# Weight differences on GpSimd, Silu at the reload, column-tile loads issued one tile further ahead

## The chip, the cores and the metric

The kernel runs on one core of one Trainium2 chip. The metric is device time in microseconds, the median of several executions. The core has a matrix engine (TensorE, PE in the profile), three elementwise engines (VectorE or DVE, ScalarE or ACT, GpSimd or POOL) and SyncE (SP), whose queue issues nearly all loads and stores between HBM and the on-chip memory SBUF. Each engine takes its own instructions strictly in order; semaphores hold one back until what it needs is there.

## What is computed

The reference is one layer of an encoder on a sequence of 1024 rows of width 1024: a token mixer with four head groups, and then a gated channel mixer (SwiGLU) of hidden width 2816. The change lies in the channel mixer:

```
for l in range(DEPTH):
    ...
    h = rms_norm(x) * (1 + sc1) + sh1
    u = h @ w_in[l]
    ...
    x = x + g1 * y
    h = rms_norm(x) * (1 + sc2) + sh2
    x = x + g2 * ((jax.nn.silu(h @ ffn_w_gate[l]) * (h @ ffn_w_up[l])) @ ffn_w_down[l])
return rms_norm(x, final_norm_g)
```

## The kernel before

The two products of the channel mixer's first half, gate and up, are done together as one two by two block product in the form of Strassen and Winograd: seven products of half-size blocks instead of eight. The hidden width is cut into 22 column tiles of 128 for the gate and 128 for the up weight; the 1024 rows are two blocks of 512 columns in a matmul. Each float32 operand is split into a high and a low part in a TensorE format: the high part is a cast on ACT (L233), the low part a subtraction on VectorE (L239), and one block product is 12 matmuls (hi·hi, hi·lo and lo·hi over four tiles of 128, L1606).

The seven products run in two loops. The **Z loop** (L1653 to L1664) makes the first two, P1 and P1 + P2, for all 22 tiles; ACT copies P1 out (L1661) and applies Silu to P1 + P2 (L1663), and both go to DRAM as psd. The **column loop** (L1716 to L1766) makes the other five for each tile f. It reloads P1 and Silu(P1 + P2) as psr (L1719), makes the weights of tile f + 1 ready, and loads two tiles x and y called sx. For f below 11 these are rows of the down weight wd, whose sums and differences are needed later (L1743, L1751, stored as td); from f = 11 on x holds results stored eleven tiles earlier (s3d, ad), and y is only written.

Making weights ready is `weights(f)`: load wg and wu (two buffers each), form four differences on VectorE (L1673, L1674, L1676, L1678) and split them into T12, T3 and t4s, high and low. The fourth difference is the last to read wg, the split T3l is the last to read wu. The results of PE leave PSUM by VectorE: L1739 and L1741 add P1 to X and Y, L1745 and L1747 add two more products, and after the product with T4 come L1754, the Silu L1755 on ACT and the multiplication L1756. L1749 forms the other half with s1, the Silu read back.

What stands where on each engine is set by a scheduler that knows priorities: `K.first()` puts what is made under it far ahead of the program's order, as far as buffers allow. A tuple of numbers at a tile names the buffers that take turns. So the weights of a tile are split about two tiles before PE uses them. After the column loop follows the down-projection (L1844, products dz, dx, dy).

Lines of the kernel that the text names:

```
def first(self):
    return self.tc.high_priority(offset=2000)
...
def split(self, hi, lo, src, hi_eng="act", lo_eng="dve"):
    ...
        nc.scalar.copy(hi, src)
    ...
    e.tensor_tensor(lo, src, hi.bitcast(F32), op=ALU.subtract)
```

Of the kernel before, what the change touches and what calls it, by code (L numbers as in the profile page):

```python
# [9 lines left out]
F32 = mybir.dt.float32  # L10
F32R = mybir.dt.float32r
AF = mybir.ActivationFunctionType
ALU = mybir.AluOpType
# [4 lines left out]
P = 128  # L18
# [3 lines left out]
NF = 22  # L22
# [263 lines left out]
def build(nc, tc, d, out, dbg=None, dump=None):  # L286
    K = Net(nc, tc, d, out)
    with ExitStack() as es:
# [93 lines left out]
        with ExitStack() as e2:  # L382
            K.pm = psum("pn", e2, m=4)
            lt = pool("lt", e2)

            rpool("edge", e2).tile([P, 120], F32, name="edge")
            rt = rpool("rt", e2)
            sp = Tags(pool("sm", e2))
            S = Slots((lt, 22), (xr, 8), (rt, 20))
            at = attention(K, sp, S)  # L390
            next(at)
            for n, ct in ((2, 6), (0, 0), (1, 4)):
                out_round(K, S, n, ct, n == 2)
            next(at)
            ffn(K, sp, S, at)
# [1186 lines left out]
def ffn(K, sp, S, at):  # L1582
# [4 lines left out]
    nc, d = K.nc, K.d  # L1587
    V = nc.vector
    H, KH = 512, NF // 2
# [11 lines left out]
    def product(ps, w, x, start):  # L1601

        n = 0
        for a, b in ((0, 0), (0, 1), (1, 0)):
            for k in range(4):
                nc.tensor.matmul(ps, lhsT=w[a][:, k], rhs=x[k][b], start=start and n == 0, stop=n == 11, skip_group_check=not start)  # L1606
                n += 1

    def pair(t, slots, name):

        hi, lo = (S.tile([P, NK, P], F32R, s, name + n) for s, n in zip(slots, "hl"))
        K.split(hi, lo, t)
        return [(hi[:, c], lo[:, c]) for c in (slice(0, 4), slice(4, 8))]

    def load(src, f, slot):
        t = S.tile([P, NK, P], F32, slot, src)
        nc.sync.dma_start(t, d[src][f])
        return t
# [36 lines left out]
    for f in range(NF):  # L1655
        with K.first():
            b11, b21 = pair(load("wg", f, W_RAW), (W_HI, W_LO), "wg")
        z = K.pg.tile([P, H], F32, "g", name="Z")
        ps1 = S.tile([P, 2, H], F32, (17, 18, 21), "ps")
        product(z, b11, A["11"], True)  # L1660
        nc.scalar.copy(ps1[:, 0], z)  # L1661
        product(z, b21, A["12"], False)
        nc.scalar.activation(ps1[:, 1], z, AF.Silu)  # L1663
        nc.sync.dma_start(K.psd[f], ps1)  # L1664


    def weights(f):
        wg, wu = load("wg", f, (22, 8)), load("wu", f, (24, 9))
        t12 = S.tile([P, NK, P], F32, (26, 10), "t12")
        t4 = S.tile([P, 4, P], F32, (19, 16), "t4")  # L1670
        B11, B21, B12, B22 = wg[:, 0:4], wg[:, 4:8], wu[:, 0:4], wu[:, 4:8]
        w = {}
        V.tensor_tensor(t12[:, 0:4], B12, B11, op=ALU.subtract)  # L1673
        V.tensor_tensor(t12[:, 4:8], B22, t12[:, 0:4], op=ALU.subtract)  # L1674
        w["T1"], w["T2"] = pair(t12, ((28, 11), (29, 14)), "T12")
        V.tensor_tensor(B12, B22, B12, op=ALU.subtract)  # L1676
        w["T3"], w["22"] = pair(wu, ((20, 12), (23, 15)), "T3")
        V.tensor_tensor(t4, B21, t12[:, 4:8], op=ALU.subtract)  # L1678
        hl = S.tile([P, 2, 4, P], F32R, (25, 13), "t4s")
        K.split(hl[:, 0], hl[:, 1], t4)  # L1680
        w["T4"] = hl[:, 0], hl[:, 1]
        return w


    def wd(k, c):
        return d["wd"][k * P:(k + 1) * P, c * H:(c + 1) * H]

    def operands(n, k):
        a, b = K.ad[k], K.ad[k + KH]
        left, right, less = ((a[:, 0:H], wd(k, 0), None), (K.sd[k][:, 0], K.td[k][:, 1], None),  # L1690
                             (b[:, 0:H], wd(k + KH, 0), None), (K.s3d[k], wd(k + KH, 1), wd(k, 1)),
                             (K.sd[k][:, 1], K.td[k][:, 0], None), (b[:, H:L], wd(k + KH, 0), K.td[k][:, 1]),
                             (K.s4d[k], wd(k + KH, 1), None))[n]
        t = S.tile([P, 2, H], F32, (22, 24, 26, 8, 9), "dr")
        nc.sync.dma_start(t[:, 0], left)
        nc.sync.dma_start(t[:, 1], right)
        if less is not None:
            m = S.tile([P, H], F32, (17, 18, 21), "dm")
            nc.sync.dma_start(m, less)
            V.tensor_tensor(t[:, 1], t[:, 1], m, op=ALU.subtract)  # L1700
        hi = S.tile([P, 2, H], F32R, (28, 20, 25, 11, 12, 13), "dh")
        lo = S.tile([P, 2, H], F32R, (29, 23, 1, 14, 15, 2), "dl")
        K.split(hi, lo, t)
        return hi, lo
# [4 lines left out]
    def more(c=1):  # L1709
        for _ in range(min(c, len(todo))):  # L1710
            with K.first():
                nk = todo.pop(0)
                ops[nk] = operands(*nk)

    with K.first():
        ws = [weights(0)]  # L1716
    for f in range(NF):
        ps1 = S.tile([P, 2, H], F32, (27, 0, 1, 2), "psr")
        nc.sync.dma_start(ps1, K.psd[f])  # L1719
        if f + 1 < NF:  # L1720
            with K.first():
                ws.append(weights(f + 1))
        else:
            more(3)
        x, y = (S.tile([P, 2, H], F32, (17, 18, 21), "sx") for _ in range(2))
        g = f % KH
        if f < KH:
            nc.sync.dma_start(x, d["wd"][f * P:(f + 1) * P].rearrange("p (b e) -> p b e", b=2))
            nc.sync.dma_start(y[:, 0], wd(f + KH, 1))
        else:  # L1730
            nc.sync.dma_start(x[:, 0], K.s3d[g])
            nc.sync.dma_start(x[:, 1], K.ad[g][:, H:L])
        w = ws[f]
        X, Y = (K.pm.tile([P, H], F32, "m", name=n) for n in "XY")
        p1, s1 = ps1[:, 0], ps1[:, 1]
        uv = S.tile([P, 2, H], F32, (3, 4), "uv")
        u, v = uv[:, 0], uv[:, 1]
        product(X, w["T2"], A["S2"], True)
        V.tensor_tensor(u, X, p1, op=ALU.add)  # L1739
        product(Y, w["T1"], A["S1"], True)  # L1740
        V.tensor_tensor(v, Y, p1, op=ALU.add)  # L1741
        if f < KH:
            V.tensor_tensor(x[:, 0], x[:, 1], x[:, 0], op=ALU.subtract)  # L1743
        product(X, w["T3"], A["S3"], False)
        V.tensor_tensor(v, X, v, op=ALU.add)  # L1745
        product(Y, w["22"], A["S4"], False)
        V.tensor_tensor(u, Y, u, op=ALU.add)  # L1747
        a = S.tile([P, L], F32, (5, 6, 7), "a")
        V.tensor_tensor(a[:, 0:H], u, s1, op=ALU.mult)  # L1749
        if f < KH:  # L1750
            V.tensor_tensor(x[:, 1], y[:, 0], x[:, 0], op=ALU.subtract)  # L1751
            nc.sync.dma_start(K.td[f], x)
        product(X, w["T4"], A["22"], False)
        V.tensor_tensor(p1, X, p1, op=ALU.add)  # L1754
        nc.scalar.activation(p1, p1, AF.Silu)  # L1755
        V.tensor_tensor(a[:, H:L], v, p1, op=ALU.mult)  # L1756
        nc.sync.dma_start(K.ad[f], a)
        if f < KH:
            V.tensor_tensor(y[:, 1], a[:, 0:H], a[:, H:L], op=ALU.subtract)
            nc.sync.dma_start(K.s3d[f], y[:, 1])  # L1760
        else:
            V.tensor_tensor(x[:, 0], a[:, H:L], x[:, 0], op=ALU.subtract)
            V.tensor_tensor(x[:, 1], x[:, 1], a[:, H:L], op=ALU.add)
            nc.sync.dma_start(K.sd[g], x)
            V.tensor_tensor(y[:, 0], a[:, 0:H], x[:, 0], op=ALU.subtract)
            nc.sync.dma_start(K.s4d[g], y[:, 0])  # L1766
# [111 lines left out]
```

## Time and profile before

| what | value |
|---|---|
| median of 3 executions | 1514.87 us (1514.78 to 1522.44) |
| profiled execution, its own time | 1520.79 us |
| its span on the core | 1518.9 us |
| mean granted TensorE clock | 0.97 |
| busy: PE, DVE, ACT, POOL | 91%, 74%, 36%, 6% |
| Z loop and column loop, roughly | 820 to 983 us, 983 to 1294 us |
| down-projection to the end | 1294 to 1519 us |

The profiled execution is one of its own, a little slower than the median. Its times place the stages; a difference between two kernels is read from the medians.

### The profile page before, as it was taken

What the parts mean: (1) busy time and instruction counts of PE and PEld (TensorE: products, weight loads), DVE (VectorE), ACT (ScalarE), POOL (GpSimd) and SP (SyncE); (2) the same over time, 40 slices, a digit from 0 to 9 for tenths busy, and PEclk for the clock granted to TensorE, in tenths of its full rate; (3) what the DMA queues carried; (4) which work ended last, traced back from release to release, by engine and by line L of the source; (5) the groups of instructions that cost most, each with busy time, mean ns of one, the idle gap of its engine ahead of it and who ended that gap; (6) DMA issues with size and microseconds to landing.
All of it is one profiled execution on the core that took longest, in us unless ns stands there. A gap on an engine that the chain in (4) does not pass through costs nothing.

```text
span 1518.9 us, 19510 instructions
## 1 busy us (share of the span) xinstructions
PE 1389.5 (91%) x6717; PEld 1115.8 (73%) x6717; DVE 1118.4 (74%) x2123; ACT 542.5 (36%) x973; POOL 90.9 (6%) x143
## 2 busy tenths in 40 slices
PE   2589989998998998999998999999999999999995
PEld 0366768776787767877776777887778878888884
DVE  7999977887756684687865458378777887557588
ACT  2522221232142342333545766322222222434352
POOL 2110000000101231320000000000000000000000
PEclk9789999999998999989999999999999999999998
DMA  6634366577662324476435448677776776977762
GB/s 248 196 101 146 121 198 217 181 240 222 205 195 93 114 84 154 118 250 223 151 102 180 146 164 285 230 258 249 254 246 218 234 266 239 331 236 244 238 221 110
DMA packets 160598, 300.31 MB, mean 198 GB/s; under 512 B 27871, under 2 KB 72831, under 8 KB 160500
## 3 DMA queue, kind: packets, MB, share of 16 engines
q1 hardware_dynamic: 137204, 271.77, 54.6%
q10 hardware_dynamic: 22688, 25.99, 4.8%
q0 software_dynamic: 608, 1.31, 0.3%
q8 instruction: 53, 0.87, 0.2%
q14 instruction: 45, 0.37, 0.1%
HBM read 221.12 MB, written 77.89 MB: 197 GB/s over the span
## 4 chain that ended last, share of the span: by engine, by line
PE 59%; DVE 14%; DMA 9%; issue 3%; ACT 1%; POOL 1%; SPq 0%; POOLq 0%; DVEq 0%; ACTq 0%
PE Z L1606 8%; PE X L1606 6%; PE dx L1844 6%; PE Y L1606 5%; PE gps L495 5%; PE gps L507 4%; PE dz L1844 4%; PE dy L1844 4%; PE gps L1556 3%; DMA mxw<-modw 3%; DMA wu<-wu 2%; PE nS L1429 2%; PE ops L1556 1%; PE nS L1407 1%; DVE wlo L239 1%
## 5 line engine op out<-in xcount | busy, mean ns | idle before, releaser
L495 PE MATMUL gps<-hhi,whi 128*128 128x512 f32 x320 | 130.3, 407 | 3.8 <-ACT nt L531 3.8
L495 PE MATMUL gps<-hlo,whi 128*128 128x512 f32 x320 | 128.9, 403 | 0.0
L495 PE MATMUL gps<-hhi,wlo 128*128 128x512 f32 x320 | 128.4, 401 | 0.0
L239 DVE TENSOR_TENSOR dl<-dr,dh 128x1024 fp32r<-128x1024 f32 x77 | 93.5, 1221 | 37.4 <-ACT dh L233 25.2
L233 ACT CAST dh<-dr 128x1024 fp32r<-128x1024 f32 x77 | 80.4, 1052 | 104.6 <-PE dz L1844 30.0
L1606 PE MATMUL Z<-hp,wgh 128*128 128x512 f32 x352 | 95.8, 402 | 1.0 <-ACT ps L1661 0.9
L507 PE MATMUL gps<-whi,hhi 128*128 128x256 f32 (+1 forms) x256 | 76.8, 300 | 1.5 <-ACT z L531 1.5
L1606 PEld LDWEIGHTS Z<-hp,wgh 128*128 128x128 f32 x352 | 63.6, 188 | 19.2 <-ACT ps L1661 4.7
L507 PE MATMUL gps<-whi,hlo 128*128 128x256 f32 (+1 forms) x256 | 76.8, 300 | 0.0
L507 PE MATMUL gps<-wlo,hhi 128*128 128x256 f32 (+1 forms) x256 | 76.3, 298 | 0.0
L495 PEld LDWEIGHTS gps<-hhi,whi 128*128 128x128 f32 x320 | 60.5, 189 | 19.3 <-ACT nt L531 5.0
L233 ACT CAST T3h<-wu 128x1024 fp32r<-128x1024 f32 x22 | 23.1, 1052 | 132.0 <-PE Y L1606 121.1
L495 PEld LDWEIGHTS gps<-hhi,wlo 128*128 128x128 f32 x320 | 60.2, 188 | 13.7 <-issue 1.6
L495 PEld LDWEIGHTS gps<-hlo,whi 128*128 128x128 f32 x320 | 60.4, 189 | 12.2 <-issue 0.8
L1500 DVE SCALAR_TENSOR_TENSOR mxacc<-mxw,cond,mxacc 128x512 f32<-128x512 f32 x56 | 41.9, 748 | 32.4 <-DMA mxw<-modw 32.2
L1606 PE MATMUL X<-A,t4s 128*128 128x512 f32 x264 | 63.6, 390 | 0.1
L1606 PEld LDWEIGHTS X<-A,t4s 128*128 128x128 f32 x264 | 49.5, 188 | 10.8 <-DVE uv L1745 0.5
L507 PEld LDWEIGHTS gps<-whi,hhi 128*128 128x128 f32 x256 | 49.9, 195 | 3.1 <-ACT z L531 1.9
L1606 PE MATMUL Y<-AS,T3h 128*128 128x512 f32 x176 | 45.5, 400 | 7.3 <-DVE uv L1741 7.3
L1844 PE MATMUL dx<-dh,dl 128*128 128x512 f32 x132 | 51.4, 389 | 0.0
L1844 PE MATMUL dx<-dh 128*128 128x512 f32 x132 | 51.4, 389 | 0.0
L1844 PE MATMUL dx<-dl,dh 128*128 128x512 f32 x132 | 51.4, 389 | 0.0
(521 smaller groups left out, 3511.2 us busy)
## 6 DMA issues: line engine op xcount, KB each, us to landing
wg<-wg SPq DMA_DIRECT2D x44, 512.0 KB
mxw<-modw SPq DMA_DIRECT2D x64, 256.0 KB
raw<-w_in SPq DMA_DIRECT2D x28, 512.0 KB
dr<-wd SPq DMA_DIRECT2D x55, 256.0 KB
psd<-ps SPq DMA_DIRECT2D x22, 512.0 KB
psr<-psd SPq DMA_DIRECT2D x22, 512.0 KB
wu<-wu SPq DMA_DIRECT2D x22, 512.0 KB
ad<-a SPq DMA_DIRECT2D x22, 512.0 KB
```

Of the source, the lines that this page charges most:

```text
L233: nc.scalar.copy(hi, src)
L239: e.tensor_tensor(lo, src, hi.bitcast(F32), op=ALU.subtract)
L495: nc.tensor.matmul(ps, lhsT=w[:, k, c], rhs=x[k][:, t], start=n == 0, stop=n == len(seq) - 1)
L507: nc.tensor.matmul(ps, lhsT=x[k][:, t], rhs=w[:, k, :N], start=n == 0, stop=n == len(seq) - 1)
L1407: nc.tensor.matmul(pb[:, :nk], lhsT=qt[r, i], rhs=ktv[r, r0:r0 + nr, f * 24:f * 24 + 40], start=True, stop=True)
L1429: nc.tensor.matmul(pb[:, 448:512], lhsT=pT[:w * 40, n], rhs=vw[:w * 40, n, c:c + 64], start=n == 0, stop=n == len(chunks) - 1)
L1500: V.scalar_tensor_tensor(acc, in0=mt, scalar=K.cond[:, k:k + 1], in1=acc, op0=ALU.mult, op1=ALU.add)
L1556: K.nc.tensor.matmul(ps, lhsT=l, rhs=r, start=n == 0, stop=n == 5)
L1606: nc.tensor.matmul(ps, lhsT=w[a][:, k], rhs=x[k][b], start=start and n == 0, stop=n == 11, skip_group_check=not start)
L1844: nc.tensor.matmul(acc[i], lhsT=a[:, 0, ts], rhs=b[:, 1], start=first and m == 0, stop=final and m == 2, skip_group_check=n in (2, 3, 5, 6))
```

## The change

Three things. The second half of the Z loop's result is copied and not put through Silu; the column loop applies Silu to it after the reload. The four weight differences are issued on GpSimd in place of VectorE. And the loads are cut out of `weights`: in iteration f the loads of wg and wu of tile f + 2 and of x and y of tile f + 1 are issued, both with priority, where it was those of f + 1 without priority for x and y. The x and y tiles get four buffers of their own in place of three, one of which is taken from psr, which keeps three of four.

```diff
--- before.py
+++ after.py
@@ -1660,22 +1660,25 @@
         product(z, b11, A["11"], True)
         nc.scalar.copy(ps1[:, 0], z)
         product(z, b21, A["12"], False)
-        nc.scalar.activation(ps1[:, 1], z, AF.Silu)
+        nc.scalar.copy(ps1[:, 1], z)
         nc.sync.dma_start(K.psd[f], ps1)


-    def weights(f):
-        wg, wu = load("wg", f, (22, 8)), load("wu", f, (24, 9))
+    def weight_loads(f):
+        return load("wg", f, (22, 8)), load("wu", f, (24, 9))
+
+    def weights(f, wg, wu):
         t12 = S.tile([P, NK, P], F32, (26, 10), "t12")
         t4 = S.tile([P, 4, P], F32, (19, 16), "t4")
         B11, B21, B12, B22 = wg[:, 0:4], wg[:, 4:8], wu[:, 0:4], wu[:, 4:8]
         w = {}
-        V.tensor_tensor(t12[:, 0:4], B12, B11, op=ALU.subtract)
-        V.tensor_tensor(t12[:, 4:8], B22, t12[:, 0:4], op=ALU.subtract)
+        G = nc.gpsimd
+        G.tensor_tensor(t12[:, 0:4], B12, B11, op=ALU.subtract)
+        G.tensor_tensor(t12[:, 4:8], B22, t12[:, 0:4], op=ALU.subtract)
         w["T1"], w["T2"] = pair(t12, ((28, 11), (29, 14)), "T12")
-        V.tensor_tensor(B12, B22, B12, op=ALU.subtract)
+        G.tensor_tensor(B12, B22, B12, op=ALU.subtract)
         w["T3"], w["22"] = pair(wu, ((20, 12), (23, 15)), "T3")
-        V.tensor_tensor(t4, B21, t12[:, 4:8], op=ALU.subtract)
+        G.tensor_tensor(t4, B21, t12[:, 4:8], op=ALU.subtract)
         hl = S.tile([P, 2, 4, P], F32R, (25, 13), "t4s")
         K.split(hl[:, 0], hl[:, 1], t4)
         w["T4"] = hl[:, 0], hl[:, 1]
@@ -1712,17 +1715,9 @@
                 nk = todo.pop(0)
                 ops[nk] = operands(*nk)

-    with K.first():
-        ws = [weights(0)]
-    for f in range(NF):
-        ps1 = S.tile([P, 2, H], F32, (27, 0, 1, 2), "psr")
-        nc.sync.dma_start(ps1, K.psd[f])
-        if f + 1 < NF:
-            with K.first():
-                ws.append(weights(f + 1))
-        else:
-            more(3)
-        x, y = (S.tile([P, 2, H], F32, (17, 18, 21), "sx") for _ in range(2))
+    def sum_loads(f):
+
+        x, y = (S.tile([P, 2, H], F32, (17, 18, 21, 2), "sx") for _ in range(2))
         g = f % KH
         if f < KH:
             nc.sync.dma_start(x, d["wd"][f * P:(f + 1) * P].rearrange("p (b e) -> p b e", b=2))
@@ -1730,9 +1725,31 @@
         else:
             nc.sync.dma_start(x[:, 0], K.s3d[g])
             nc.sync.dma_start(x[:, 1], K.ad[g][:, H:L])
+        return x, y
+
+
+    with K.first():
+        loaded = weight_loads(0)
+        ws = [weights(0, *loaded)]
+        loaded = weight_loads(1)
+        xy = sum_loads(0)
+    for f in range(NF):
+        ps1 = S.tile([P, 2, H], F32, (27, 0, 1), "psr")
+        nc.sync.dma_start(ps1, K.psd[f])
+        x, y = xy
+        g = f % KH
+        if f + 1 < NF:
+            with K.first():
+                ws.append(weights(f + 1, *loaded))
+                if f + 2 < NF:
+                    loaded = weight_loads(f + 2)
+                xy = sum_loads(f + 1)
+        else:
+            more(3)
         w = ws[f]
         X, Y = (K.pm.tile([P, H], F32, "m", name=n) for n in "XY")
         p1, s1 = ps1[:, 0], ps1[:, 1]
+        nc.scalar.activation(s1, s1, AF.Silu)
         uv = S.tile([P, 2, H], F32, (3, 4), "uv")
         u, v = uv[:, 0], uv[:, 1]
         product(X, w["T2"], A["S2"], True)
```

The rows that follow stand in the order of one engine's queue, each with its line, its tiles (numbered when they are made) and, in brackets, for whose semaphores it waits. Line numbers of after differ: psr load L1738 (was L1719), x L1723 and y L1724 (L1728, L1729), differences L1676, L1677, L1679, L1681, L1756 (L1739), L1758 (L1741), L1760 (L1743), L1762 (L1745), L1764 (L1747), L1766 (L1749), L1768 (L1751), L1771 (L1754), L1772 (L1755), L1773 (L1756), stores L1769, L1774, L1777, L1781, L1783 (L1752, L1757, L1760, L1764, L1766); L1752 is the new Silu.

SP's queue in the first half of the column loop, before:

```order
L1719 DMA psr_9460<-psd6_162 128x1024 [waits DMAHW7_49,Activation_49]
L1728 DMA sx_9273<-wd 128x1024 [waits DMAHW6_49,DMAHW0_49]
L1617 DMA wg_9567<-wg 128x1024 [waits DMAHW1_49,DVE_49]
L1752 DMA td3_181<-sx_9168 128x1024 [waits DMAHW3_49,DVE_49]
L1617 DMA wu_9464<-wu 128x1024 [waits DVE_49]
L1729 DMA sx_9274<-wd 128x512 [waits DMAHW4_49,DMAHW2_49]
L1757 DMA ad3_133<-a_9228 128x1024 [waits DMAHW5_49,DVE_49]
L1760 DMA s3d3_203<-sx_9169 128x512 [waits DVE_49]
```

and of the change:

```order
L1617 DMA wu_9283<-wu 128x1024 [waits DVE_49]
L1723 DMA sx_9285<-wd 128x1024 [waits DMAHW6_49,DMAHW4_49]
L1774 DMA ad2_132<-a_9134 128x1024 [waits DVE_49]
L1777 DMA s3d2_202<-sx_8968 128x512 [waits DMAHW0_49,DVE_49]
L1617 DMA wg_9493<-wg 128x1024 [waits DMAHW1_49,Pool_49]
L1738 DMA psr_9368<-psd5_161 128x1024 [waits DMAHW2_49,Activation_49]
L1724 DMA sx_9180<-wd 128x512 [waits DMAHW3_49,DMAHW0_49]
L1769 DMA td4_182<-sx_9179 128x1024 [waits DVE_49]
L1617 DMA wu_9389<-wu 128x1024 [waits DMAHW5_49,DVE_49]
```

The wg load waited for VectorE and now waits for POOL; the psr load and the load of y (L1724) have moved behind it.

VectorE's queue over one tile in the first half, before:

```order
L1739 TENSOR_TENSOR uv_9384<-X_9382,psr_9355 128x512 [waits PE_49]
L1673 TENSOR_TENSOR t12_9571<-wu_9569,wg_9567 128x512 [waits DMAHW3_49,DMAHW1_49]
L1759 TENSOR_TENSOR sx_9274<-a_9333 128x512 [waits DMAHW2_49,DVE_49]
L1674 TENSOR_TENSOR t12_9571<-wu_9569,t12_9571 128x512 [waits DVE_49]
L239 TENSOR_TENSOR T12l_9471<-t12_9466,T12h_9470 128x1024 [waits PE_49,Activation_49]
L1676 TENSOR_TENSOR wu_9569<-wu_9569 128x512
L1678 TENSOR_TENSOR t4_9572<-wg_9567,t12_9571 128x512 [waits DVE_49]
L1741 TENSOR_TENSOR uv_9384<-Y_9383,psr_9355 128x512
L1751 TENSOR_TENSOR sx_9378<-sx_9379,sx_9378 128x512 [waits DMAHW4_49]
L1745 TENSOR_TENSOR uv_9384<-X_9382,uv_9384 128x512 [waits DVE_49,PE_49]
L1747 TENSOR_TENSOR uv_9384<-Y_9383,uv_9384 128x512 [waits PE_49]
L239 TENSOR_TENSOR T3l_9476<-wu_9464,T3h_9475 128x1024 [waits Activation_49]
```

and of the change:

```order
L1756 TENSOR_TENSOR uv_9186<-X_9183,psr_9156 128x512 [waits PE_49]
L1760 TENSOR_TENSOR sx_9285<-sx_9285 128x512 [waits DMAHW6_49,DMAHW4_49]
L1758 TENSOR_TENSOR uv_9186<-Y_9184,psr_9156 128x512 [waits PE_49]
L239 TENSOR_TENSOR T12l_9269<-t12_9264,T12h_9268 128x1024 [waits Activation_49]
L1762 TENSOR_TENSOR uv_9186<-X_9183,uv_9186 128x512 [waits DVE_49,PE_49]
L1768 TENSOR_TENSOR sx_9179<-sx_9180,sx_9179 128x512 [waits DMAHW3_49]
L1764 TENSOR_TENSOR uv_9186<-Y_9184,uv_9186 128x512 [waits PE_49]
L239 TENSOR_TENSOR T3l_9274<-wu_9177,T3h_9273 128x1024 [waits Activation_49]
L1766 TENSOR_TENSOR a_9240<-uv_9186,psr_9156 128x512 [waits DMAHW7_49,DVE_49]
L1771 TENSOR_TENSOR psr_9156<-X_9183,psr_9156 128x512 [waits PE_49]
L239 TENSOR_TENSOR t4s_9278<-t4_9265,t4s_9278 128x512 [waits Activation_49]
```

The four differences and the wait of the first for wu and wg are gone; L1768, which waits for the load of y of the next tile, stands ahead of L1764 and T3l, as L1751 stood ahead of L1747. That is so in tiles 2 to 4 and 6 to 8; in the other tiles of the first half but the first L1768 stands behind T3l.

ACT's queue over one tile in the second half, before:

```order
L233 CAST T3h_10315<-wu_10304 128x1024 [waits DMAHW3_49,PE_49,Activation_49]
L233 CAST t4s_10320<-t4_10307 128x512 [waits PE_49,Activation_49]
L1755 ACTIVATE psr_10195<-psr_10195 128x512 [waits DMAHW6_49,DVE_49]
L233 CAST T12h_10415<-t12_10411 128x1024 [waits PE_49,Activation_49]
L233 CAST T3h_10420<-wu_10409 128x1024 [waits DMAHW3_49,PE_49,Activation_49]
```

and of the change:

```order
L233 CAST T12h_10328<-t12_10324 128x1024 [waits PE_49,Pool_49]
L233 CAST T3h_10333<-wu_10237 128x1024 [waits DMAHW2_49,PE_49,Pool_49]
L1752 ACTIVATE psr_10428<-psr_10428 128x512 [waits DMAHW1_49,DVE_49]
L233 CAST t4s_10338<-t4_10325 128x512 [waits PE_49,Pool_49]
L1772 ACTIVATE psr_10216<-psr_10216 128x512 [waits DVE_49]
```

The new Silu, of psr two tiles ahead, stands ahead of the cast t4s and of the Silu of P1 (L1772, before L1755) and waits for a load. SP's queue there, of the change:

```order
L1617 DMA wg_10447<-wg 128x1024 [waits DMAHW5_49,Pool_49]
L1783 DMA s4d0_211<-sx_9922 128x512 [waits DMAHW6_49,DVE_49]
L1726 DMA sx_10133<-s3d2_202 128x512 [waits DMAHW7_49,DMAHW4_49]
L1727 DMA sx_10133<-ad2_132 128x512 [waits DMAHW0_49]
L1738 DMA psr_10322<-psd14_170 128x1024 [waits DMAHW1_49,Activation_49]
L1617 DMA wu_10343<-wu 128x1024 [waits DMAHW2_49,DVE_49]
```

psr stands behind wg, which waits for POOL, a store and the two loads of x.

## Rows read from the trace of the kernel before

**Rows 1.** Busy time, share and instructions by engine; POOL's busy tenths in 40 slices.

```profile
PE 1389.5 (91%) x6717; PEld 1115.8 (73%) x6717; DVE 1118.4 (74%) x2123; ACT 542.5 (36%) x973; POOL 90.9 (6%) x143
...
POOL 2110000000101231320000000000000000000000
```

**Rows 2.** Chain that ended last: start, us, engine or transfer.

```profile
1082.83 4.15 DMA wu<-wu
...
1096.98 4.93 DMA wu<-wu
...
1111.93 4.62 DMA wu<-wu
...
1294.23 29.92 PE dz L1844 x132
```

**Rows 3.** PE's timeline at the fourth product of tiles 0, 11 and 21.

```profile
990.55 2.00 PE L1606 MATMUL Y<-AS,T3h 128*128 128x512 f32 x8
...
1150.43 2.11 PE L1606 MATMUL Y<-AS,T3h 128*128 128x512 f32 x8 [0.35 <-DVE uv L1741]
...
1288.63 1.98 PE L1606 MATMUL Y<-AS,T3h 128*128 128x512 f32 x8
```

**Rows 4.** Waits from 979 to 1300: us in total, times, longest.

```profile
PE Y L1606 <- DVE uv L1741: 7.3, 9, 1.2
DVE t L1673 <- DMA wu<-wu: 7.0, 9, 1.2
```

**Rows 5.** VectorE's timeline in a tile of the first half.

```profile
1095.63 1.22 DVE L239 TENSOR_TENSOR T3l<-wu,T3h 128x1024 fp32r<-128x1024 f32 x1
...
1102.00 0.69 DVE L1673 TENSOR_TENSOR t<-wu,wg 128x512 f32<-128x512 f32 x1 [1.06 <-DMA wu<-wu]
...
1106.15 0.68 DVE L1741 TENSOR_TENSOR uv<-Y,psr 128x512 f32<-128x512 f32 x1
```

**Rows 6.** SP's timeline, three loads in a row, and VectorE at their last reader.

```profile
1001.96 0.33 SPq L1617 DMA_DIRECT2D wg<-wg  x1
...
1002.83 0.42 SPq L1728 DMA_DIRECT2D sx<-wd  x1
...
1008.32 0.69 DVE L1743 TENSOR_TENSOR sx<-sx 128x512 f32<-128x512 f32 x1 [0.76 <-DMA sx<-wd]
```

**Rows 7.** POOL's groups by line: count, busy us, mean ns, idle before.

```profile
L239 POOL TENSOR_TENSOR hlo<-tm,hhi 128x512 fp32r<-128x512 f32 x8 | 11.9, 1492 | 47.3 <-DVE hhi L235 47.3
...
L429 POOL TENSOR_TENSOR acc<-acc,pr 128x512 f32<-128x512 f32 x7 | 10.1, 1449 | 13.6 <-ACT pr L427 13.3
L1349 POOL TENSOR_TENSOR mhh<-mtt,mnd 128x512 f32<-128x512 f32 x8 | 9.2, 1152 | 44.8 <-DVE mnd L1347 44.8
```

**Rows 8.** Timelines of POOL and VectorE where two subtractions overlap.

```profile
74.16 1.64 POOL L239 TENSOR_TENSOR hlo<-tm,hhi 128x512 fp32r<-128x512 f32 x1 [0.70 <-DVE hhi L235]
...
74.60 2.28 DVE L239 TENSOR_TENSOR wlo<-raw,whi 128x1024 fp32r<-128x1024 f32 x1
```

**Rows 9.** ACT's groups by line: count, busy us, mean ns, idle before.

```profile
L1755 ACT ACTIVATE psr<-psr 128x512 f32<-128x512 f32 x22 | 13.9, 633 | 3.3 <-DVE psr L1754 2.4
L233 ACT CAST t4s<-t 128x512 fp32r<-128x512 f32 x22 | 13.7, 621 | 55.0 <-PE X L1606 54.9
L1663 ACT ACTIVATE ps<-Z 128x512 f32<-128x512 f32 x22 | 13.1, 593 | 3.2 <-PE Z L1606 3.1
L1661 ACT COPY ps<-Z 128x512 f32<-128x512 f32 x22 | 12.9, 585 | 9.0 <-issue 6.1 <-PE Z L1606 1.3 <-ACT ps L1663 1.0
...
L1663 ACT ACT_TABLE_LOAD x6 | 7.7, 1283 | 0.1
```

**Rows 10.** Windows: length, busy us (instructions) by engine, granted clock, DMA share, GB/s.

```profile
806.00:808.00 2.00, 2.00 (x12) 2.00 (x12) 1.89 (x5) 0.28 (x2) 0.00 (x0) 0.50 0.71 291
...
860.00:880.00 20.00, 20.00 (x109) 15.63 (x107) 8.50 (x30) 11.26 (x28) 0.00 (x0) 1.00 0.26 93
1060.00:1080.00 20.00, 17.86 (x78) 14.14 (x77) 15.45 (x23) 3.46 (x5) 0.00 (x0) 1.00 0.75 246
```

**Rows 11.** PE's timeline ahead of the windows at half clock.

```profile
802.38 0.65 PE L1421 MATMUL nT<-ident,nsb 128*120 128x128 f32 x4 [3.15 <-ACT nsb L1417]
```

## The prediction

> **What bounds the kernel now.** First the busy shares [rows 1]: TensorE (PE) is busy 91% of the span, VectorE (DVE) 74%, GpSimd (POOL) 6%, and POOL's line of slices is empty from the middle on, so where the change puts work on POOL nothing else runs there. Then the chain that ended last [rows 2]: the down-projection runs 132 matmuls in 29.92 us, 0.2267 us each, which is what PE needs when nothing holds it up. A column tile has five products of 12 matmuls, so at that rate it takes 60 × 0.2267 = 13.6 us. The timeline of PE at the fourth product of a tile [rows 3] shows what a tile takes: from tile 0 to tile 11 1150.43 − 990.55 = 159.9 us, where 11 × 13.6 = 149.6 would do, and from tile 11 to tile 21 138.2 where 136.0 would do. So the column loop, the only place that the change reaches with any weight, loses about 10.3 us in its first half and 2.2 in its second. That is the whole prize: 12.5 us, 0.8% of the time.
>
> The waits [rows 4] and VectorE's timeline [rows 5] say what loses it. PE waits nine times for the copy-out L1741, 7.3 us in all; VectorE waits nine times for wu at L1673, 7.0 us. VectorE runs its instructions in order: T3l (to 1096.85) frees the wu buffer, wu is loaded in 4.93 us [rows 2], L1673 starts at 1102.00, and only behind it and the rest of the differences stands L1741 (1106.15), for which PE waits. That is a loop one tile long, 14.5 to 15 us, a little over PE's 13.6.
>
> **The change part by part.** *Silu.* At L1663 a Silu of 593 ns becomes a copy like that of L1661, 585 ns [rows 9], and six table loads of 1.28 us go. They buy nothing: in that stage PE is busy 20.00 of 20 us [rows 10], so ACT's time lies beside full products. In the column loop ACT gets a Silu per tile, priced by L1755 at 633 ns; ACT is busy 3.46 of 20 us there [rows 10], so its length is hidden. Its place is not: it waits for a load, and t4s and the Silu of L1772 are queued behind it.
>
> *Differences.* Four instructions of 0.68 us per tile leave VectorE (2.7 of about 11.6 us), and the wait for wu leaves with them. So the old loop is gone. On POOL the same form (128x512 float32, two full operands) shows 1.449 us in the mean at L429; the least of the bounds is 1.152, the mean of L1349, and at the other end L239 with 1.492 [rows 7], stretched where it meets VectorE to 1.64 [rows 8]. I take 1.45, the nearest row: 5.8 us per tile, bounds 4.6 to 6.6. POOL has 13.6 us for it, so its throughput does not bind. What counts is who is queued behind the last of them.
>
> *Loads one tile ahead.* The buffers are still two for wg and two for wu, so a load issued earlier in the program does not start earlier: it waits in SP's queue for its buffer, and everything after it on SP waits too. The rows of the order, in the section on the change, show what: wg of tile f+3 now waits for POOL, because the fourth difference is the last to read the old wg; behind it stand psr and the second wd load, y; and VectorE meets y at L1768 before it gets to L1764 and to T3l, which frees the next wu. So a new loop closes in the first half, one tile long:
>
> T3l ends; 0.1 us to the issue; wu 4.6 us [rows 2]; four differences 5.8; wg, psr and y land. Of three loads issued together, 1.25 MB, the last reader started 6.4 us after the first issue [rows 6], one load alone takes 4.6 to 4.9; I take 5.7 between them, 4.9 where y stands directly behind wg. Then L1768, L1764 and T3l, 0.68 + 0.68 + 1.22 = 2.6. Sum 0.1 + 4.6 + 5.8 + 5.7 + 2.6 = 18.8 us, against 13.6 for PE (18.0 in the short form).
>
> The loop acts only where L1768 of the next tile stands before T3l, which by the order is in two runs of three tiles, 2 to 4 and 6 to 8. A run has some slack before PE feels it: T3l ends nominally 24 matmuls, a copy-out and itself after the third product began (5.4 + 0.7 + 1.2 = 7.3 us), and from there to the next tile's third product six VectorE instructions (4.0 us) are needed, 11.3 of 13.6, so 2.3 us once per run. A run costs (18.0 − 13.6) + 2 × (18.8 − 13.6) − 2.3 = 12.5 us. Two runs: 25.0. At the start of the column loop x of tile 0 is queued on SP behind a wg that waits for POOL, which I estimate at 2.5 us from the same terms. First half: 27.5 lost instead of 10.3, **+17.2**.
>
> In the second half no y is loaded, but psr is, and it stands behind wg, the s4d store and two x loads. ACT's new Silu waits for psr, and t4s and L1772 wait behind it. That closes a loop two tiles long: 0.1 + wu 4.6 + POOL 5.8 + wg to psr landed (1.75 MB; the slope between one load and three gives 6.9 to 7.4, taken 6.9) + Silu 0.63 + t4s 0.62 + L1772 0.63 + five VectorE instructions 3.4 + 7.3 to the next T3l = 30.0 us, 15.0 per tile. Against 13.6 that is 1.4 × 9 tiles = 12.6, less the 2.3 of slack, instead of 2.2: **+8.1**.
>
> The down-projection and everything before the column loop keep their order; nothing is added for them. Sum +25.3: from the median of 1514.87 to **1540**. The profiled execution took 1520.79 (span 1518.9) and was the slow side of the three runs, so a profile of the change as slow as that one would show 1546.
>
> *A page against the rows.* A VectorE subtraction of 1.22 us elsewhere took 2.28 where it overlapped a subtraction on POOL that itself took 1.64 [rows 8]: the two hold each other up. The Trainium skill, page SBUF — State Buffer, section Who interferes with whom, says that a VectorE instruction with two SBUF inputs and a GpSimd instruction that reads SBUF share one port as an exclusive lock, the later one blocking fully; the row agrees in sign, and by that rule rival 3 follows.
>
> **Rivals.** 1. *The other side: the new loop closes inside PE's time.* Only 4.2 us per load (the shortest in [rows 2] is 4.15), 4.6 for the differences and 4.2 for y give 0.1 + 4.2 + 4.6 + 4.2 + 2.6 = 15.7, and the slack of 2.3 then covers a run almost wholly; the second loop gives 26.5, below 27.2. Then the 12.5 us of stalls go but for some 2.5 at the start: 1505. The mechanism is that VectorE no longer stands in front of L1741 waiting for wu; for it speaks that VectorE then needs about 9 of 13.6 us. It decides below about 14.5 us of the one-tile loop. Against it: 5.7 is nearer to the measured three loads than 4.2. Chance 0.22.
>
> 2. *Stalls exchanged.* A loop of 16.5 to 17 us costs 4 to 6 per run, 10 to 12 in the first half, and the second half is where it was: 1510 to 1520, 1515 in the middle. Chance 0.18.
>
> 3. *The lock.* POOL's differences are stretched by VectorE's subtractions to 1.64 and more, and T3l and T12l by POOL's as in [rows 8]. With 7.0 instead of 5.8, and 0.8 more in T3l, the loop is 20.8, a run costs 18.5, the second loop 31.8: about 37 + 2.5 − 10.3 + 18.4 − 2.2 − 2.3 = +43, 1558. For it: VectorE remains busy with two-input subtractions two thirds of the time. Against it: copy-outs read PSUM and one SBUF operand, and the 1.449 is a mean with VectorE at work. Chance 0.12.
>
> 4. *The clock.* After PE had stood for 3.15 us [rows 11] the granted clock was 0.50, 1.2 GHz, in the following windows [rows 10]. The stalls I expect are 4 to 5 us long where the loop acts; each could cost some 3.5 us more over 7 us at half rate. Before, stalls of 1.2 us left the clock at 1.00 [rows 10]. This comes on top of the forecast: with 6 such stalls 1561. Chance 0.08.
>
> **How the numbers follow.** Forecast (1523 to 1550) 0.4; rival 1 0.22; rival 2 0.18; rivals 3 and 4 together 0.2. A measurement of this kernel can tell about 0.5%, 7.6 us, from no change: 1507.3 to 1522.4 is the same. Faster 0.22 (rival 1), same 0.18 (rival 2), slower 0.6 (the rest). The range for 8 in 10 leaves out the lower half of rival 1 and the upper half of rivals 3 and 4: 1505 to 1558. The likeliest case, slower, has its own range of 1523 to 1558.
>
> **What would show it.** Right: four POOL instructions per tile at 1.3 to 1.6 us; SP waiting at L1617 for POOL; VectorE waiting at L1768 for the wd load, several us, in two runs of three tiles with tiles of 17 to 19 us between them; ACT waiting at L1752 for psr in the second half, tiles near 15; PE waiting for L1756, L1762 or L1764; the 29.92 us of the down-projection unchanged. L1673's wait must be gone from VectorE. Wrong: if y lands before VectorE comes to L1768 (then rival 1), if PE's tiles are 13.6 in both halves, if the POOL instructions are over 2 us, or if time is lost in the stage before the column loop, where copies replace Silu.

## The result and the profile after

The changed kernel takes 1585.01 us in the median of six executions, the kernel before, measured beside it, 1517.15. One of the six was disturbed (3483.98); the other five lie between 1581.75 and 1585.93, their median is 1584.22, and the ratio leaves the sixth out: 1.0434, 95% interval 1.0411 to 1.0458. Slower was forecast, but 1540, and at most 1558. The profiled execution took 1585.79, its span is 1584.0, 65.1 longer than before.

The busy times of the page, and POOL's slices [rows 1]:

```profile
PE 1412.1 (89%) x6717; PEld 1130.7 (71%) x6717; DVE 1106.6 (70%) x2035; ACT 543.5 (34%) x988; POOL 228.8 (14%) x231
...
POOL 2110000000103213300000032333334330000000
```

Two numbers stand out. PE is busy 22.6 us longer for the same 6717 matmuls: it ran slower. And VectorE lost 88 instructions of 0.68 us, 60 us, but is busy only 11.8 us less: the rest got 48 us longer.

PE's timeline at the fourth product of tiles 0, 11 and 21, as in [rows 3], and at the third and fourth of tile 12:

```profile
990.96 1.98 PE L1606 MATMUL Y<-AS,T3h 128*128 128x512 f32 x8
...
1177.36 1.98 PE L1606 MATMUL Y<-AS,T3h 128*128 128x512 f32 x8
...
1192.17 3.75 PE L1606 MATMUL X<-AS,T3h 128*128 128x512 f32 x8 [3.77 <-DVE uv L1756]
...
1197.42 2.11 PE L1606 MATMUL Y<-AS,T3h 128*128 128x512 f32 x8
...
1349.58 1.98 PE L1606 MATMUL Y<-AS,T3h 128*128 128x512 f32 x8
```

The first half of the column loop takes 186.4 us where it took 159.9 [rows 3]; the second 172.2 where it took 138.2. With 4.1 more from there to the second product of the down-projection that is nearly the whole difference. The windows of the two halves (columns as in [rows 10]), before and then after, show how much of it is slower work:

```profile
990.55:1150.43 159.88, 152.68 (x662) 123.13 (x661) 127.10 (x185) 36.98 (x44) 0.00 (x0) 1.00 0.73 250
1150.43:1288.63 138.20, 137.43 (x599) 112.02 (x600) 110.81 (x158) 33.73 (x40) 0.00 (x0) 1.00 0.70 239
...
990.96:1177.36 186.40, 160.79 (x662) 129.14 (x660) 118.69 (x143) 41.67 (x55) 69.01 (x45) 0.95 0.61 217
1177.36:1349.58 172.22, 148.60 (x605) 119.44 (x604) 115.87 (x130) 38.31 (x49) 45.87 (x29) 0.92 0.55 196
```

Of the 26.5 us lost in the first half 8.1 are PE's longer busy time, of the 34.0 in the second 11.2; the rest is waiting. After the stall of 3.77 us at 1192.17 a product of 12 matmuls takes 5.25 us (to 1197.42), where 2.72 is PE's own rate. The windows around it, and one further on, show the clock that goes with it:

```profile
1180.00:1200.00 20.00, 16.23 (x61) 12.90 (x60) 11.50 (x13) 4.04 (x6) 6.85 (x4) 0.83 0.46 167
...
1194.00:1196.00 2.00, 2.00 (x6) 1.60 (x5) 0.86 (x1) 0.00 (x0) 1.99 (x1) 0.50 0.00 0
...
1280.00:1300.00 20.00, 15.93 (x58) 12.94 (x59) 13.47 (x15) 3.00 (x5) 5.04 (x4) 0.75 0.50 179
```

0.50 is the lower of the clock's two levels, 1.2 GHz in place of 2.4; the windows of 20 us mix the two.

Three waits that were forecast are there (from 979 to 1365, columns as in [rows 4]): ACT's for psr (28.7 of its 98.5 us between 1175 and 1330, in the second half), PE's for L1756 and VectorE's for y.

```profile
ACT psr L1752 <- DMA psr<-psd: 98.5, 18, 12.8
...
PE X L1606 <- DVE uv L1756: 47.8, 16, 6.8
DVE sx L1768 <- DMA sx<-wd: 35.1, 9, 7.0
```

So is the loop forecast for the first half. Rows of SP, POOL and VectorE from one T3l to the next:

```profile
1054.07 0.33 SPq L1617 DMA_DIRECT2D wu<-wu  x1
...
1057.61 1.27 POOL L1676 TENSOR_TENSOR t<-wu,wg 128x512 f32<-128x512 f32 x1 [11.96 <-DMA wu<-wu]
...
1061.95 2.28 POOL L1681 TENSOR_TENSOR t<-wg,t 128x512 f32<-128x512 f32 x1
...
1064.26 0.33 SPq L1617 DMA_DIRECT2D wg<-wg  x1
...
1069.66 0.69 DVE L1768 TENSOR_TENSOR sx<-sx 128x512 f32<-128x512 f32 x1 [5.99 <-DMA sx<-wd]
1070.27 0.68 DVE L1764 TENSOR_TENSOR uv<-Y,uv 128x512 f32<-128x512 f32 x1
1070.87 1.21 DVE L239 TENSOR_TENSOR T3l<-wu,T3h 128x1024 fp32r<-128x1024 f32 x1
...
1072.12 0.33 SPq L1617 DMA_DIRECT2D wu<-wu  x1
```

wu lands 3.5 us after its issue, the four differences take 6.6, wg to y 5.4, the rest 2.5: 18.05 us from wu to wu, where 18.8 was forecast. In the second half psr stands on the chain that ended last every second tile, as the forecast loop of two tiles has it:

```profile
1197.94 5.11 DMA psr<-psd
...
1209.05 1.74 DVE sx L1782
...
1211.54 4.47 PE X L1606 x12
...
1232.36 5.58 DMA psr<-psd
...
1269.22 5.46 DMA psr<-psd
```

But two tiles take 34.4 and then 36.9 us, where 30.0 was forecast. Rows of VectorE and then of POOL from there show what was not forecast:

```profile
1205.64 1.79 DVE L1779 TENSOR_TENSOR sx<-a,sx 128x512 f32<-128x512 f32 x1
1207.35 1.78 DVE L1780 TENSOR_TENSOR sx<-sx,a 128x512 f32<-128x512 f32 x1
1209.05 1.74 DVE L1782 TENSOR_TENSOR sx<-a,sx 128x512 f32<-128x512 f32 x1
1210.71 0.68 DVE L1756 TENSOR_TENSOR uv<-X,psr 128x512 f32<-128x512 f32 x1
...
1205.59 1.28 POOL L1676 TENSOR_TENSOR t<-wu,wg 128x512 f32<-128x512 f32 x1 [9.60 <-DMA wu<-wu]
1206.95 1.62 POOL L1677 TENSOR_TENSOR t<-wu,t 128x512 f32<-128x512 f32 x1
```

wu lands when VectorE is between L1773 and L1756, and the three subtractions there take 1.74 to 1.79 us each in place of 0.68. L1756, for which PE waits, is 3.3 us later for that alone. L1756 itself keeps its 0.68, though POOL's four differences go on beside it to 1211.92: it reads one operand from PSUM and only one from SBUF.

### The profile page after: what moved, and what is told of

Same layout as the page of the kernel before. It is cut to its first block, busy times and chain, and to the rows that moved or that the text cites. A ratio compares the mean times of both kernels' runs of the same rounds, so it can differ in the third digit from the quotient of the medians.

```text
span 1584.0 us, 19585 instructions
## 1 busy us (share of the span) xinstructions
PE 1412.1 (89%) x6717; PEld 1130.7 (71%) x6717; DVE 1106.6 (70%) x2035; ACT 543.5 (34%) x988; POOL 228.8 (14%) x231
## 5 line engine op out<-in xcount | busy, mean ns | idle before, releaser
L1606 PE MATMUL Z<-hp,wgh 128*128 128x512 f32 x352 | 98.5, 411 | 4.5 <-ACT ps L1661 4.3
L1606 PE MATMUL X<-AS,T3h 128*128 128x512 f32 x176 | 58.8, 489 | 47.8 <-DVE uv L1756 47.8
L1676 POOL TENSOR_TENSOR t<-wu,wg 128x512 f32<-128x512 f32 x22 | 31.9, 1452 | 477.5 <-DMA wu<-wu 318.9
L1606 PEld LDWEIGHTS X<-AS,T3h 128*128 128x128 f32 x176 | 40.6, 240 | 63.2 <-issue 48.9
L239 DVE TENSOR_TENSOR wgl<-wg,wgh 128x1024 fp32r<-128x1024 f32 x22 | 28.1, 1280 | 38.2 <-ACT wgh L233 36.1
```

The source lines that it names most:

```text
L1676: G.tensor_tensor(t12[:, 0:4], B12, B11, op=ALU.subtract)
```

## The experiments

Theory A: SP's queue stands still at the wg load until GpSimd has done its fourth difference, and psr and y stand behind it. Theory B: GpSimd's reads hold up VectorE's subtractions. Rival C: the earlier loads and the third psr buffer do the harm. Rival D: ACT's new wait for psr does. Each time below is a median in us, with its ratio to the kernel before, measured beside it (1516 to 1520), and the 95% interval of the ratio.

**One part at a time.** Loads alone, that is the change with Silu back in the Z loop and the differences back on VectorE:

```diff
-        nc.scalar.copy(ps1[:, 1], z)
+        nc.scalar.activation(ps1[:, 1], z, AF.Silu)
...
-        G = nc.gpsimd
+        G = nc.vector
...
-        nc.scalar.activation(s1, s1, AF.Silu)
```

> Only the loads are issued one tile earlier (with the buffers that this takes); differences stay on VectorE, Silu stays at the Z loop. Theory A (the time is lost because wg waits for GpSimd and psr and y stand behind it): no GpSimd, so no such wait: 1510 to 1525 us. Theory B (GpSimd's reads hold up VectorE's subtractions): the same, 1510 to 1525. Rival C (the earlier loads and the third psr buffer alone do the harm): 1550 or more.

Measured: 1517.80, 0.9985 (0.9965 to 1.0005). The loads by themselves cost nothing. Next the differences alone, the kernel before with `nc.gpsimd.tensor_tensor` in the four lines:

> Only the four differences go to GpSimd; loads and Silu as before. The order still has wg waiting for GpSimd and psr and the second wd load behind it. Theory A: most of the loss is here, 1550 to 1580 us. Theory B: VectorE's stretched instructions come too, 1550 to 1580. Rival C: 1510 to 1525, since the loads are not moved.

Measured: 1574.92, 1.0373 (1.0348 to 1.0398), as both theories have it. Silu alone, at the reload:

> Only the Silu moves from the Z loop to the reload. Theories A and B: 1512 to 1520 us, no difference; TensorE is busy all the time in the Z loop, and with four psr buffers the reload is early. Rival D (ACT waiting for psr in front of t4s is a loss by itself): 1525 or more.

Measured: 1518.94, 1.0018 (0.9991 to 1.0044). The change with `G = nc.vector`:

> The whole change, but the four differences on VectorE. Theories A and B: nearly all of the 68 us come back, 1510 to 1530 us. Rival C: 1550 or more.

Measured: 1520.11, 1.0026 (1.0007 to 1.0045). C and D fall: all but 2 or 3 us of the loss go with the differences' engine. Alone in the kernel before that engine costs 57 us, in the change 65: the moved loads, which cost nothing by themselves, seem to add some 8 to it.

**The reads by themselves.** The base is the kernel before with `(27, 0, 1), "psr"`:

> The kernel before with three psr buffers in place of four, and nothing else: the base for the next two. Both theories: 1513 to 1523 us.

Measured: 1518.77, 0.9988 (0.9958 to 1.0018). On this base, work on GpSimd that no instruction of the column loop waits for:

```diff
         nc.sync.dma_start(K.ad[f], a)
+        idle = S.tile([P, H], F32, 2, "idle")
+        for _ in range(4):
+            nc.gpsimd.tensor_tensor(idle, a[:, 0:H], a[:, H:L], op=ALU.subtract)
```

> The base, and in each column tile GpSimd subtracts the two halves of a four times into a buffer that nobody reads, once a is done. No load waits for these. Theory A (the queue behind the wg load): 1513 to 1525 us. Theory B (GpSimd's reads hold up VectorE's two-input subtractions, some 3 us per tile): 1555 to 1590, with VectorE's 128x512 subtractions at 1.7 us in place of 0.68 where they overlap.

Measured: 1633.64, 1.0761 (1.0717 to 1.0804), 44 us above theory B's range. And the same with fills in place of the four subtractions:

```diff
+        nc.gpsimd.tensor_tensor(idle[:, 0:8], a[:, 0:8], a[:, H:H + 8], op=ALU.subtract)
+        for _ in range(11):
+            nc.gpsimd.memset(idle, 0.0)
```

> As the one before, but GpSimd only fills the buffer, eleven times per tile, about as long, after one subtraction of 8 columns that sets the moment. It writes and hardly reads. Theories A and B: 1513 to 1525 us, VectorE's subtractions at 0.68 us. If VectorE is stretched here too, it is not the reading.

Measured: 1516.80, 0.9986 (0.9960 to 1.0012). VectorE's order in the column loop is the same in both. Timeline of POOL and VectorE in the run with reads:

```profile
1114.85 6.36 POOL L1760 TENSOR_TENSOR idle<-a 128x512 f32<-128x512 f32 x4 [12.52 <-DVE a L1756]
...
1116.61 1.78 DVE L1762 TENSOR_TENSOR sx<-a 128x512 f32<-128x512 f32 x1
1118.31 1.77 DVE L1674 TENSOR_TENSOR t<-wu,t 128x512 f32<-128x512 f32 x1
1120.01 1.75 DVE L1676 TENSOR_TENSOR wu<-wu 128x512 f32<-128x512 f32 x1
```

and in the run with fills:

```profile
1110.38 6.37 POOL L1761 MEMSET idle<- 128x512 f32 x11
...
1112.82 0.68 DVE L1763 TENSOR_TENSOR sx<-a 128x512 f32<-128x512 f32 x1
1113.42 0.68 DVE L1674 TENSOR_TENSOR t<-wu,t 128x512 f32<-128x512 f32 x1
```

POOL is about as long at work in both, 6.7 us per tile with reads and 6.4 with fills in the mean. Only the reads lengthen VectorE, by 1.1 us per subtraction, and four reads per tile cost 115 us, more than the change. Most of the held-up subtractions stand between the copy-outs L1739 and L1741, and PE waits for L1741, with reads and then with fills:

```profile
PE Y L1606 <- DVE uv L1741: 60.4, 15, 4.2
...
PE Y L1606 <- DVE uv L1741: 8.2, 8, 1.6
```

PE's busy time with reads is 1434.3 us, 45.5 more than in the base, for the same matmuls.

**The queue by itself.** psr, x and y of the change by `nc.scalar.dma_start`:

> The whole change, with psr, x and y loaded by ACT's queue, so that they no longer stand behind the wg load; the differences stay on GpSimd. Theory A: the loop through the queue is open, 1520 to 1540 us, and VectorE's wait at L1768 is gone. Theory B: VectorE stays stretched, 1550 to 1575.

Measured: 1554.45, 1.0223 (1.0187 to 1.0259). VectorE's wait at L1768 is gone (0.4 us in all), as theory A has it, but the time lies in theory B's range. The same with `G = nc.vector`:

> As the run with ACT's queue, but the differences on VectorE: neither the reads of GpSimd nor the queue. Against that run (1554 us) this is the price of GpSimd's work without the queue: theory B says 30 to 45 us, so 1510 to 1524. If the rest of the loss were ACT's loads and the Silu: 1540 or more.

Measured: 1535.21, 1.0114 (1.0076 to 1.0152), outside both ranges: ACT's queue costs about 15 us of its own (1520.11 with the same loads on SP's), so this pair shows only that GpSimd costs 19 there, where it costs 65 on SP's queue. Next, psr with priority and `xy = sum_loads(f + 1)` ahead of the weight loads:

> The whole change, with psr loaded with priority and x and y issued in the program before wg and wu: in the order psr now stands ahead of the wg load everywhere, while y still stands behind it, but VectorE comes to y (L1768) mostly after T3l. Theory A for the queue's part: most of the 30 us that ACT's queue gave back come back here too, 1550 to 1565 us; the rest, from GpSimd's reads, stays. If the queue's part is all at y: 1575 or more.

Measured: 1596.01, 1.0517 (1.0474 to 1.0560), more than the change itself. The order was not the expected one: psr was ahead of wg, but in the first half wu now stood behind y, y behind an s3d store and that behind wg; SP waited 131 us for GpSimd. So this run does not say where the queue's part lies. Only the fourth difference on GpSimd (`nc.gpsimd` in that line, `G = nc.vector` for the others):

> The whole change, but only the fourth difference on GpSimd, three on VectorE. Theory B: one read per tile instead of four, about a quarter of the held-up time, 1523 to 1540 us. Theory A alone (wg waits for GpSimd in any case, only the sum of the loop is shorter): 1520 to 1530.

Measured: 1540.52, 1.0133 (1.0093 to 1.0174), just above theory B's range and clear of theory A's. A quarter of the reads costs 20 us of the 65. Three wg buffers, `load("wg", f, (22, 8, 2))`, on the change, for which x and y go back to three:

> The whole change with three wg buffers (x and y go back to three). The wg load then waits for the fourth difference of the tile before, long done, so nothing on SP stands still for GpSimd, while GpSimd reads as much as before. If the loss is mostly the queue: 1525 to 1545 us. If it is mostly the held-up subtractions: 1560 or more. The wait of SP's L1617 for GpSimd should fall from 85 us to under 20 either way.

Measured: 1581.14, 1.0392 (1.0355 to 1.0430). And on the differences alone, with three psr buffers:

> Only the differences on GpSimd, with three wg buffers (and three of psr): loads and Silu as before. Against the run with the differences alone (1575 us): if the queue is most of it 1520 to 1545, if the held-up subtractions are 1555 or more.

Measured: 1575.07, 1.0356 (1.0327 to 1.0385). Both times lie in the range that was to speak for the subtractions, but neither tells the theories apart: the loads were only issued one tile earlier, and SP waited as before. Its wait (us, times, longest) in the run on the change:

```profile
SPq L1617 <- POOL t L1681: 93.5, 18, 7.7
```

In the change it is

```profile
SPq L1617 <- POOL t L1681: 84.9, 18, 8.7
```

The wait without the reads, eleven `nc.gpsimd.memset(B21, 0.0)` behind the fourth difference on VectorE:

> The change with its differences on VectorE, and GpSimd then fills the half of wg that the fourth difference has read, eleven times, before the next wg load may start: the wait of SP for GpSimd without the reads. (The filled data are used by nothing.) In the order psr and y stand ahead of the wg load here, stores behind it. If any wait of SP for GpSimd is dear: 1545 or more. If it is dear only with psr or y behind it: 1520 to 1535.

Measured: 1521.32, 1.0032 (1.0002 to 1.0063). SP waits for GpSimd 27.5 us, and nothing is lost against the change with its differences on VectorE (1520.11). But this wait is a third of the change's, and psr and y stand ahead of the wg load here. No run has them behind it, as in the change, without GpSimd's reads. Last, the wait taken off SP while the reads stay:

```diff
-        return load("wg", f, (22, 8)), load("wu", f, (24, 9))
+        wg = S.tile([P, NK, P], F32, (22, 8), "wg")
+        nc.gpsimd.dma_start(wg, d["wg"][f])
+        return wg, load("wu", f, (24, 9))
```

> The whole change, with the wg loads of the column loop issued by GpSimd itself, right behind its fourth difference. SP's order is that of the change without the wg loads, so nothing on SP waits for GpSimd, while GpSimd reads as in the change. If the loss is mostly SP's queue standing still: 1525 to 1545 us, no wait of SP for GpSimd and none of several us at L1768. If it is mostly the held-up subtractions: 1555 or more, with VectorE's subtractions as long as in the change. The time between them is the share of each.

Measured: 1547.35, 1.0189 (1.0121 to 1.0257). VectorE's busy time, 1102.8 us, is nearly that of the change, so the reads still hold it up. SP's longest waits are now

```profile
SPq L1617 <- DVE T3l L239: 67.2, 19, 8.1
SPq L1700 <- DVE dl L239: 46.3, 27, 4.6
```

and for GpSimd it waits only 5.8 us, at loads of the down-projection. The time lies between the two stated cases, so both causes have a share: 1585 − 1547 = 38 us for the queue; 1547 − 1520 (all on VectorE) = 27 us for the reads. The interval of this run makes each uncertain by some 10 us.

**A third wu buffer.** The kernel before, with `load("wu", f, (24, 9, 2))` and three psr buffers:

> The kernel before with three wu buffers in place of two and three psr buffers in place of four; differences on VectorE. If the wait for wu at L1673 is what holds L1741 up, it goes, and the column loop loses 7 to 10 us: 1507 to 1511 us against 1518. If something else is late by as much: 1515 to 1520.

Measured: 1511.17, 0.9959 (0.9933 to 0.9984), less than either kernel. PE's timeline:

```profile
1099.44 1.98 PE L1606 MATMUL X<-AS,T3h 128*128 128x512 f32 x8
1113.04 1.98 PE L1606 MATMUL X<-AS,T3h 128*128 128x512 f32 x8
1126.64 1.98 PE L1606 MATMUL X<-AS,T3h 128*128 128x512 f32 x8
```

A tile of the first half is 13.60 us, PE's own rate, and of the 7.3 us for which PE waited at L1741 [rows 4] 0.2 are left; a tile of the second half is 13.9, as before. By the medians 8.5 us are won, by the interval 2 to 10, of the 12.5 that the column loop had to give.

## Why the prediction was right and wrong

*What bounds the kernel* was right: a third wu buffer removes the loop through L1673, and the first half of the column loop, where that loop cost most, then runs at 13.6 us. *Silu and its table loads* were worth nothing, as said. *The first-half loop* was right in its links and nearly in its length, 18.05 us for 18.8: shorter loads made up for longer differences. Its price was forecast at 17.2 us over before and is 26.5. From tile 0 to tile 2 the kernel lost 10.0 us, at 17.9 and 19.3 a tile, where 2.5 was allowed for the start; the rest of the half lost 26.8, where the two runs of the forecast lose 25.0.

*The step that failed* is the sum for the second half: forecast +8.1, measured +34.0. A loop two tiles long with psr in it was there, but the sum has "five VectorE instructions 3.4", at 0.68 each. Three of them, L1779, L1780 and L1782, stand where wu lands and POOL starts to read. In seven tiles they took 30.4 us (rows below) where 21 × 0.68 = 14.3 would do: 16 us more. Another 11.2 are PE's slower products. 8.1 + 16 + 11.2 = 35 comes near the 34.0; that these terms simply add is an estimate.

The lock had been put into a rival with a chance of 0.12, on a row that showed it (2.28 for 1.22, [rows 8]). There it stretched only T3l and the differences in the sum, and T12l without a price. T3l was hardly touched, T12l took 1.80 us in place of 1.22, and the subtractions ahead of L1756 were left out. By line, VectorE's mean in the change from 990 to 1310 (columns as in [rows 7]):

```profile
L239 DVE TENSOR_TENSOR T12l<-t,T12h 128x1024 fp32r<-128x1024 f32 x19 | 34.3, 1803 | 0.0
L239 DVE TENSOR_TENSOR T3l<-wu,T3h 128x1024 fp32r<-128x1024 f32 x19 | 23.1, 1217 | 4.7 <-ACT T3h L233 4.7
...
L1782 DVE TENSOR_TENSOR sx<-a,sx 128x512 f32<-128x512 f32 x7 | 12.3, 1757 | 0.0
L1756 DVE TENSOR_TENSOR uv<-X,psr 128x512 f32<-128x512 f32 x18 | 12.2, 680 | 0.0
...
L1780 DVE TENSOR_TENSOR sx<-sx,a 128x512 f32<-128x512 f32 x7 | 10.2, 1456 | 0.0
...
L1779 DVE TENSOR_TENSOR sx<-a,sx 128x512 f32<-128x512 f32 x7 | 7.9, 1122 | 0.2
```

The Trainium skill, page SBUF — State Buffer, section Who interferes with whom, names just this border: two SBUF inputs contend with a GpSimd instruction that reads, one input does not, and a GpSimd instruction that only writes does not. The rows agree in all three: 1757 ns, 680 ns, and 0.68 us beside fills.

*The clock*, rival 4, was right in kind: the windows with the longer stalls show 0.75 to 0.91 where those of before show 1.00, and PE's 22.6 us more for the same matmuls are about a third of the loss. Of PE's sixteen stalls for L1756, nine, of 2.5 to 6.8 us, were followed by eight matmuls in 3.3 to 3.75 us; after the other seven, of up to 2.8 us, they took 2.1 at most. The clock was kept out of the likeliest sum, though that sum had stalls of 4 to 5 us in it; this is the second error of size.

Rivals 1 and 2 fell: y landed 6 us after VectorE was ready for it in the row at 1069.66, and late nine times in all. Two of the rivals' sums do not come out. By its own 15.7, rival 1 still pays 3 × 2.1 − 2.3 = 4.0 us per run, and its 26.5 takes a shorter landing of psr than it names. Rival 3 adds 18.4 for a second loop of 31.8, where nine tiles at 2.3 make 20.7. The result turns on neither.

The down-projection keeps its 29.92 us per group, but loses 4.1 at its first. In the change with all on VectorE that is 6.0 and with the loads alone 2.8, so it comes with the loads.

The change's 68 us are thus 65 of the differences' engine and 2 to 3 of the other parts. Most of PE's slower products go with the queue's wait: PE is busy 1412.1 us in the change, 1397.5 with wg loaded by GpSimd and 1393.7 with all on VectorE. The split of 38 and 27 is not exact, and not only for the interval: the reads lengthen the four differences too (6.4 us per tile in the mean, 5.1 undisturbed), so part of the queue's share is theirs, and the wg load by GpSimd may have a price of its own. On ACT's queue the reads cost 19.

## What to carry to other kernels

Before work moves to an idle engine, ask which instructions of the busy one will meet it, and whether they stand ahead of the copy-out that TensorE waits for: a subtraction of two SBUF operands that takes 0.68 us alone takes 1.75 beside a read on GpSimd. Ask of every load which engine frees its buffer, and what is queued behind that load; a wait in an in-order queue is paid by the loads behind it, and a buffer more only helps if the order does not use it to issue earlier. A stall of 3.8 us cost 2.5 more here, because the clock fell with it, so a forecast with such stalls needs the slower products in its sum.

## What was not expected of the hardware

GpSimd's subtraction and VectorE's take turns, each until the other's is done. In the rows of the second half L1779 ends at 1207.43, POOL's L1677 at 1208.57 and L1780 at 1209.13. So 1.28 us alone becomes 1.6 to 2.28 on GpSimd, and 0.68 becomes 1.75 on VectorE. Four such reads per column tile, needed by nothing, cost 115 us; eleven fills of nearly the same total length cost nothing that can be measured.
